# Where the quarter sums of FFN weights are made: DRAM copies against accumulating transfers into SBUF

## The chip, the cores and the metric

The kernel runs on one core of a Trainium2 chip. The metric is the device time of one execution in microseconds (us), in the median of several runs. Of each kernel one execution is also profiled; its span, from the first to the last instruction of the program, is what the views of the profile divide up.

The engines are PE (matrix products, with PEld for the loading of their weights), DVE (elementwise on 128 partitions), ACT (scalar functions, and the casts here), POOL and SP. In this kernel POOL makes almost no arithmetic: it issues DMAs, among them all that add to what lies at their target (`accum_op=add`), and SP issues the plain loads. Each engine executes its own instructions in order, so a DMA that has to wait holds up every later DMA of the engine that issues it.

## The reference

Two layers over 512 latent and 256 context tokens of width 1024, in float32. Layer 0 is windowed attention, layer 1 retention; each is followed by a SwiGLU network of inner width 2816:

```python
def swiglu(h, w_in, w_out):
    gate, up = jnp.split(h @ w_in, 2, axis=-1)
    return (jax.nn.silu(gate) * up) @ w_out

for i in range(DEPTH):
    mx = jnp.split(c_act @ ada_w[i] + ada_b[i], 6, axis=-1)      # latent modulation
    mc = jnp.split(cc_act @ ada_w[i] + ada_b[i], 6, axis=-1)     # context modulation
    h_x = modulate(rms_norm(x, norm1_g[i]), mx[0], mx[1])
    ...                                                          # mixer i, gated residual
    x = x + mx[5] * swiglu(modulate(rms_norm(x, norm2_g[i]), mx[3], mx[4]), ffn_w_in[i], ffn_w_out[i])
    if need_ctx_out:                                             # layer 0 only
        y_ctx = y_ctx + mc[5] * swiglu(...)
```

The change touches the feed-forward network of layer 0 (768 tokens, latent and context side by side) and the modulation vectors of layer 1, which are worked out while it runs.

## The kernel before, in words

Every matrix product is made of three float32r products (high times high, low times high, high times low). So each weight and each activation is split first: ACT casts the high part (L171), DVE subtracts it to get the low part (L172). These two lines appear all over the profile.

**Stages, in order.** Modulation and projections of layer 0 (to about 105 us), attention in 24 blocks, four groups of heads with six blocks each (about 105 to 310), the attention's output projection, the first two column tiles of the feed-forward network in the plain way, then the part around the change: **the run** of gate and up tiles 2 to 21 (about 402 to 705), **the output products** of the same network (705 to 883), then retention and the second network.

**The run.** `w_in` is cut into 22 column tiles of 128 gate and 128 up columns. A tile of gate and up is a 2x2 block matrix: the input `wgu` holds its quarters as gate top (0), gate bottom (1), up top (2), up bottom (3), each 128 x 512 (256 KB). `seven(pos, jobs)` (L1164) computes a tile with 7 products instead of 8, each of 12 matmuls with 384 token columns. For that it needs the quarters, and sums of them. Two sums of raw quarters come from DRAM buffers `gu_sum`: gate top plus up top, loaded to the tile `t1raw` by `load_sum`, and up top plus up bottom, loaded to the left half of a `wraw` tile by `load_up`, whose right half is up bottom. `load_gate` loads both gate quarters. The other sums are DVE additions (L1149, L1155). `t1raw` has one buffer; the three kinds of `wraw` loads go round three buffers, so each load waits on SP until DVE has finished with the buffer's former content.

Where in a tile each load is issued: `load_up(pos + 1)` after the split of the gate tile (`b24`), `load_gate(pos + 2)` after the split of the up tile (`b3`), `load_sum(pos + 2)` after the split of `t1raw` for tile pos + 1. After every second tile `pair_sums` sends four results (`saved`, L1069 and L1071) to DRAM from POOL.

**The sums in DRAM.** `gu_sum` has four batches of five tiles. A batch is two copies (`sum_copy`, L827) and two accumulating DMAs (`sum_add`, L830), 1280 KB each. The output weights need four sums of quarters, `fo_sum`, in two batches of six and five pairs: per batch four copies and four accumulating DMAs (1536 or 1280 KB). `spread` assigns each DMA a turn: turns 0 to 23 are the blocks of attention, -1 is before them, 100 + pos is a tile of the run. The `gu_sum` batches and the first `fo_sum` batch are made before and during attention, the second `fo_sum` batch in the run, from POOL, at tiles 4 (two copies), 6 and 8 (accumulating), 10 (copy), 12 (accumulating), 14 (copy) and 16 (accumulating).

**The order of work.** Outside the run a planner orders the instructions by simulated costs; `after` gives it an order to keep, and puts no wait on the chip. In the run and the output products (`with tc.manual_schedule`, L1453) the order on all engines is the order of the program text.

**The modulation tiles.** Layer 1's modulation is 48 tiles: `ada_next` multiplies a 512 KB weight tile `adaw` with the condition vector on DVE (L284), twice (latent and context) for every second entry of the list from the first on until there are 16 such, once for all others, and `ada_ahead` issues the load of the next tile at once. `adaw` has one buffer, so the load of the next tile waits for the DVE operation on the last, and the next operation waits for that load. In the run the load is issued by SP, in the output products by POOL. `seven` calls two jobs that may be `ada_next`: `jobs[0]` after its third product and `jobs[2]` at the end of the tile. Tiles 5 to 21 have it at `jobs[2]`; all of them but 7, 9, 13 and 17 also have it at `jobs[0]`. That is 30 modulation tiles in the run; the other 18 are done in the output products.

**The output products.** Seven products (prod 0 to 6) of six steps (m 0 to 5), 24 matmuls of 384 columns in a step and 12 in the last. In each step `fo_split` splits the weights and tokens of the step after next on ACT and DVE (2 splits), then the step's matmuls are issued, and then a modulation tile at m = 0, 2 and 4 of prods 0 to 4 and at m = 3 of prods 0 to 3, until none is left. At the end of most products `fo_add` adds the banks to the streams (L1285).

Of the kernel before, what the change touches and what calls it, by code (L numbers as in the profile page):

```python
# [8 lines left out]
F32 = mybir.dt.float32  # L9
# [5 lines left out]
P = 128  # L15
# [9 lines left out]
FFN_GROUPS = (2, 4, 4, 4, 4, 4)  # L25
PAIRS = FT // 2
TURN = [p + PAIRS * j for p in range(PAIRS) for j in range(2)]
GU_BATCH, GU_BATCHES = 5, 4
ROW = 2048
FO_BATCHES = (6, 5)  # L30
RH = 4
# [23 lines left out]
def dit_kernel(ctx, tc, xT, cT, crow, small, consts, masks, tabs0, tabs1, jtab, adaQ, adaN, adaT, wst, wgu, wfo, out):  # L55
    nc = tc.nc
    mult, add, sub = ALU.mult, ALU.add, ALU.subtract
# [38 lines left out]
    by_hand = [False]  # L96

    def after(ins, others):
        for o in others if not by_hand[0] else ():
            tc.add_manual_dep(ins.ins, o.ins.name, order, reason="table set turn")  # L100
# [719 lines left out]

    dp = ctx.enter_context(tc.tile_pool(name="dp", bufs=1, space=bass.MemoryType.DRAM))
    flat = lambda t: t.rearrange("a p n -> (a p n)").rearrange("(x y) -> x y", y=2048)
    gu_sum = [dp.tile([2, GU_BATCH, P, 512], F32, name=f"gu_sum{b}") for b in range(GU_BATCHES)]
    fo_sum = [dp.tile([4, n, P, 512], F32, name=f"fo_sum{b}") for b, n in enumerate(FO_BATCHES)]

    def sum_copy(dst, src, behind):
        after((nc.gpsimd if by_hand[0] else nc.sync).dma_start(flat(dst), flat(src), max_dma_last_dim=ROW), [behind] if behind else [])  # L827

    def sum_add(dst, src, behind):
        after(nc.gpsimd.dma_start(flat(dst), flat(src), accum_op=add, max_dma_last_dim=ROW), [behind] if behind else [])  # L830

    def gu_steps(b):
        rows = slice(2 + b * GU_BATCH, 2 + (b + 1) * GU_BATCH)
        t = gu_sum[b]
        return [lambda a: sum_copy(t[0], wgu[0, rows], a), lambda a: sum_copy(t[1], wgu[2, rows], a),
                lambda a: sum_add(t[0], wgu[2, rows], a), lambda a: sum_add(t[1], wgu[3, rows], a)]

    def fo_steps(b):
        rows = slice(sum(FO_BATCHES[:b]), sum(FO_BATCHES[:b + 1]))
        t = fo_sum[b]  # L840
        return [lambda a: sum_copy(t[3], wfo[0, rows], a), lambda a: sum_copy(t[2], wfo[2, rows], a),
                lambda a: sum_add(t[3], wfo[2, rows], a), lambda a: sum_add(t[2], wfo[3, rows], a),
                lambda a: sum_copy(t[0], t[3], a), lambda a: sum_add(t[0], wfo[3, rows], a),
                lambda a: sum_copy(t[1], t[0], a), lambda a: sum_add(t[1], wfo[1, rows], a)]
# [3 lines left out]
    def spread(steps, turns):  # L848
        for st, n in zip(steps, turns):
            sum_turns.setdefault(n, []).append(st)  # L850

    spread(gu_steps(0), (-1, -1, 0, 1))
    spread(gu_steps(1), (-1, -1, 2, 3))
    spread(gu_steps(2), (4, 4, 6, 7))
    spread(gu_steps(3), (8, 8, 9, 10))
    spread(fo_steps(0), (11, 11, 13, 14, 16, 17, 19, 21))
    spread(fo_steps(1), (104, 104, 106, 108, 110, 112, 114, 116))

    for st in sum_turns[-1]:
        st(keys_end)  # L860
    for piece in make_q(1):
        piece()
    rope_key(kn[2])
# [255 lines left out]
    def ada_next(behind=()):  # L1119

        args = ada_q.pop(0)
        ada_tile(*args, cr, behind, fp, ada_w.pop())
        ada_ahead()
# [12 lines left out]
    def load_up(pos):  # L1136
        u = tile[pos]["u"] = raw_turn()
        nc.sync.dma_start(u[:, R_], wgu[3, pos])
        nc.sync.dma_start(u[:, L_], gu_sum[(pos - 2) // GU_BATCH][1, (pos - 2) % GU_BATCH])

    def load_sum(pos):
        t = tile[pos]["t"] = T(fp, 512, "t1raw", 1)
        nc.sync.dma_start(t, gu_sum[(pos - 2) // GU_BATCH][0, (pos - 2) % GU_BATCH])

    def split_gate(pos):
        t = tile[pos]
# [306 lines left out]
    with tc.manual_schedule(engines=Hand):  # L1453
        by_hand[0] = True
        for pos in range(2, FT):
            jobs = [nothing] * 3
            if pos == 2:
                jobs = [last_sum, gates_negated, nothing]
            elif pos == 3:
                jobs[0] = rows_begin  # L1460
            elif pos == 4:
                jobs[2] = rows_silu
                ada_ahead()
            else:
                cr = row_t[0]
                jobs[2] = ada_next
                if pos not in (7, 9, 13, 17):
                    jobs[0] = ada_next
            if pos == FT - 1:
                def begin():  # L1470
                    fo_split_weights(0)
                    fo_split_tokens(0)
                    fo_split_tokens(1)
                jobs[1] = begin
            end = seven(pos, jobs)
            for st in sum_turns.get(100 + pos, ()):
                st(None)
        fo_y = [bank("Y"), bank("Z"), bank("Z"), bank("Y")]
        o = fo_y
        for i, (prod, m) in enumerate(FO):  # L1480
            if m == 0 and prod:
                o = fo_y if prod in (2, 4) else fo_z if prod == 5 else [bank("X"), bank("X"), pj(384), pj(384)] \
                    if prod in (1, 3) else [bank("Y"), bank("Z"), bank("Z"), bank("Y")]
                if prod == 3:
                    fo_z = o
            if i == 0:
                fo_split_weights(1)
                last_gate(FT - 1)
            if i + 2 < len(FO) and i + 4 != len(FO) and i + 3 != len(FO):
                fo_split(i + 2)  # L1490
            last = i == len(FO) - 2
            fo_step(i, o, prod in (0, 1, 3, 6), last)
            if m == (PAIRS - 1) // 2:
                for args in (((0, 0),), ((0, 0),), ((4, 0, True),), ((4, 1),), ((4, 1, True), (0, 1)), ((4, 0),), ())[prod]:
                    fo_add(o, *args)
            if prod < 5:
                ada_next() if ada_q and (m % 2 == 0 or m == 3 and prod < 4) else None
            elif prod == 5:
                early_sums(m)
            else:  # L1500
                late_sums(m)
            if last:
                break
            if i == 2:
                Q.close()
                H = ExitStack()
                hpool[0] = H.enter_context(tc.tile_pool(name="hR", bufs=1, reuse_waits="tile", side="right"))
                h_rest += [(T(hpool[0], 512, "aq", 11, F32R), T(hpool[0], 512, "aq", 11, F32R)) for _ in range(4)]
                h_first += [T(hpool[0], 512, "aq", 11, F32R) for _ in range(3)]
                off_grid(hpool[0], 16)  # L1510
                h_first.insert(0, T(hpool[0], 512, "aq0", 1, F32R))
                hm += [T(hpool[0], 512, "qk", 8) for _ in range(KT)]
        fo_add(o, 0, 1)
        last_square = last_squares()
        b11.append(split_chunk(b11.pop()))
        by_hand[0] = False
# [778 lines left out]
```

## Time and profile before

| | us |
|---|---|
| median of 3 runs (lowest, highest) | 1723.99 (1723.61, 1726.64) |
| profiled execution | 1723.45 |
| its span | 1721.4 |
| run, from the copy of the first product of tile 2 to that of tile 21 | 404.4 to 693.1 |
| output products 0 to 4 | 705.2 to 834.0 |

Reading: in the views below a row of a group is line, engine, operation, written tile, read tiles, form, how many; then busy us and mean ns of one; then the idle time of the engine just before them and what ended it. A row of waits is engine and what it was to do, `<-` what ended the wait, then us in total, how often, and the longest. A row of windows is from:to, its length, the busy us of PE, PEld, DVE, ACT and POOL with the number of their instructions, the share of full clock granted to PE, the busy share of the 16 DMA engines, and GB/s. PE's busy time is modelled for pipelined matmuls, so lost time is best read as the length of a stretch against that of an undisturbed one with the same work.

### The profile page before, as it was taken

What the parts mean: (1) busy time and instruction counts of PE and PEld (TensorE: products, weight loads), DVE (VectorE), ACT (ScalarE), POOL (GpSimd) and SP (SyncE); (2) the same over time, 40 slices, a digit from 0 to 9 for tenths busy, and PEclk for the clock granted to TensorE, in tenths of its full rate; (3) what the DMA queues carried; (4) which work ended last, traced back from release to release, by engine and by line L of the source; (5) the groups of instructions that cost most, each with busy time, mean ns of one, the idle gap of its engine ahead of it and who ended that gap; (6) DMA issues with size and microseconds to landing.
All of it is one profiled execution on the core that took longest, in us unless ns stands there. A gap on an engine that the chain in (4) does not pass through costs nothing.

```text
span 1721.4 us, 27879 instructions
## 1 busy us (share of the span) xinstructions
PE 1684.6 (98%) x10798; PEld 1523.2 (88%) x10798; DVE 1341.1 (78%) x2395; ACT 891.7 (52%) x1565; POOL 104.5 (6%) x223
## 2 busy tenths in 40 slices
PE   8999999999999999999999999999999999999999
PEld 5878877899999999998988888898898899999997
DVE  6788888797778778776899857757757898877874
ACT  5678878474444334433565535534524564444442
POOL 0011111000101001100000000000000000000000
PEclk9999999999999999999999999999999999999999
DMA  9848967644786777788763624625724323333322
GB/s 382 310 91 195 239 141 190 220 153 141 252 237 231 227 215 227 269 269 286 253 182 72 195 90 120 182 61 132 192 65 100 122 74 113 109 110 111 98 87 86
DMA packets 112035, 293.86 MB, mean 171 GB/s; under 512 B 9520, under 2 KB 20288, under 8 KB 111648
## 3 DMA queue, kind: packets, MB, share of 16 engines
q1 hardware_dynamic: 88960, 227.67, 40.3%
q0 software_dynamic: 22656, 63.90, 16.2%
q8 instruction: 84, 1.38, 0.3%
q10 hardware_dynamic: 288, 0.52, 0.1%
q14 instruction: 47, 0.39, 0.1%
HBM read 274.82 MB, written 61.28 MB: 195 GB/s over the span
## 4 chain that ended last, share of the span: by engine, by line
PE 44%; DVE 6%; DMA 3%; issue 1%; ACT 1%; POOL 0%; DVEq 0%; ACTq 0%; SPq 0%; POOLq 0%
PE Y L971 6%; PE Z L1597 6%; PE Z L971 3%; PE Y L1586 3%; PE pj L154 2%; PE pj L156 2%; PE pj L155 2%; DMA adaw<-in_adaT_dram 2%; PE pj L1597 2%; PE X L971 2%; PE X L1586 1%; DVE wlo L172 1%; DMA wraw<-in_wst_dram 1%; PE X L1597 1%; PE Z L1266 1%
## 5 line engine op out<-in xcount | busy, mean ns | idle before, releaser
L171 ACT CAST whi<-wraw 128x1024 fp32r<-128x1024 f32 (+1 forms) x284 | 294.3, 1040 | 314.3 <-PE Y L971 70.6
L172 DVE TENSOR_TENSOR wlo<-wraw,whi 128x1024 fp32r<-128x1024 f32 (+1 forms) x284 | 342.4, 1209 | 102.1 <-ACT whi L171 101.0
L971 PE MATMUL Y<-aq,whi 128*128 128x384 f32 x640 | 172.8, 335 | 0.0
L284 DVE CUSTOM_DVE_ANT_0 y<-adaw,crow,small_sb 128x1024 bf16<-128x1024 f32 x64 | 82.1, 1283 | 59.0 <-DMA adaw<-in_adaT_dram 58.4
L971 PEld LDWEIGHTS Y<-aq,whi 128*128 128x128 f32 x640 | 116.7, 188 | 0.0
L971 PE MATMUL Y<-aq,wlo 128*128 128x384 f32 x320 | 107.8, 337 | 8.6 <-DVE wlo L172 8.6
L1597 PE MATMUL Z<-whi,sA 128*128 128x512 f32 x256 | 80.6, 392 | 0.0
L108 ACT ACTIVATE pr<-pr,stat,qs 128x513 f32<-128x513 f32 (+2 forms) x96 | 74.1, 774 | 11.3 <-DVE stat L734 11.3
L154 PE MATMUL pj<-ax,whi 128*128 128x512 f32 x176 | 69.2, 393 | 0.5 <-DVE res L263 0.3
L971 PEld LDWEIGHTS Y<-aq,wlo 128*128 128x128 f32 x320 | 60.2, 188 | 10.5 <-DVE wlo L172 10.5
L156 PE MATMUL pj<-ax,whi 128*128 128x512 f32 x176 | 68.7, 390 | 0.0
L155 PE MATMUL pj<-ax,wlo 128*128 128x512 f32 x176 | 68.6, 390 | 0.0
L971 PE MATMUL Y<-sA,whi 128*128 128x256 f32 x304 | 58.3, 277 | 0.0
L263 DVE SCALAR_TENSOR_TENSOR res<-pj,mod,res 128x512 f32<-128x512 f32 (+1 forms) x64 | 45.3, 713 | 16.6 <-PE pj L156 16.6
L753 PE MATMUL pT<-const_sb,pr 128*128 128x128 f32 x352 | 56.4, 285 | 1.8 <-DVE pr L744 1.1
L728 DVE CUSTOM_DVE_ANT_0 pr<-S,mask,qs 128x256 f32<-128x256 f32 (+1 forms) x96 | 53.3, 567 | 5.3 <-PE S L727 4.4
L1597 PEld LDWEIGHTS Z<-whi,sA 128*128 128x128 f32 x256 | 48.0, 188 | 10.5
L971 PE MATMUL Y<-hx,whi 128*128 128x256 f32 x304 | 56.4, 277 | 0.0
L1266 PE MATMUL Y<-aq,whi 128*128 128x384 f32 x176 | 53.4, 340 | 1.6 <-DVE aq L172 1.4
L1266 PE MATMUL Z<-aq,whi 128*128 128x384 f32 x176 | 51.5, 334 | 0.0
L753 PEld LDWEIGHTS pT<-const_sb,pr 128*128 128x128 f32 x352 | 41.2, 145 | 11.0 <-issue 4.3
L1597 PE MATMUL Z<-wlo,sA 128*128 128x512 f32 x128 | 50.5, 395 | 0.0
(602 smaller groups left out, 5089.4 us busy)
## 6 DMA issues: line engine op xcount, KB each, us to landing
wraw<-in_wst_dram SPq DMA_DIRECT2D x157, 512.0 KB, 3.7
adaw<-in_adaT_dram SPq DMA_DIRECT2D x35, 512.0 KB, 3.7
op<-saved SPq DMA_DIRECT2D x35, 384.0 KB, 5.4
saved<-op POOLq DMA_DIRECT2D x33, 384.0 KB, 4.1
wraw<-in_wgu_dram SPq DMA_DIRECT2D x24, 512.0 KB, 4.5
adaw<-in_adaT_dram POOLq DMA_DIRECT2D x21, 512.0 KB, 4.2
gu_sum<-in_wgu_dram SPq DMA_DIRECT2D x8, 1280.0 KB, 12.6
gu_sum<-in_wgu_dram POOLq DMA_DIRECT2D x8, 1280.0 KB, 12.8
```

The costliest lines, as they stand in the source:

```text
L108: ins = nc.scalar.activation(*args, **kw)
L154: nc.tensor.matmul(o, whi, xhi, start=first, stop=False)
L155: nc.tensor.matmul(o, wlo, xhi, start=False, stop=False)
L156: return nc.tensor.matmul(o, whi, xlo, start=False, stop=last)
L171: after(nc.scalar.copy(hi, t), behind)
L172: return nc.vector.tensor_tensor(lo, t, hi, op=sub)
L284: res.append(nc.vector.tensor_tensor_reduce(junk, w, cr[:, s * 1024:(s + 1) * 1024], 1.0, sm_t[:, C_ADAB + l * 48 + j:C_ADAB + l * 48 + j ...
L753: nc.tensor.transpose(tp[:, a * P:(a + 1) * P], self.pr[(0, 2, 1, 3)[a]][:, ki * P:(ki + 1) * P], ident)
L971: nc.tensor.matmul(o, p, r, start=first and k + i == 0, stop=k == 3 and i == 2, skip_group_check=not first)
L1266: nc.tensor.matmul(o[d], p[:, ws], r, start=first and k + e == 0, stop=k == PAIRS - 1 and e == 2, skip_group_check=True)
L1586: ins = nc.tensor.matmul(o[:, e * SC:(e + 1) * SC], p[:, ws], r, start=first and k + e + i == 0, stop=k == 3 and i == 2, skip_group_check= ...
L1597: ins = nc.tensor.matmul(os[t], p, r, start=first and k + i == 0, stop=k == 3 and i == 2, skip_group_check=by_k or not first)
```

## The change

1. `gu_sum`, its four batches (16 DMAs of 1280 KB) and `gu_steps` are gone. In the run `load_up` and `load_sum` load the raw quarter instead (`wgu[2]` and `wgu[0]`, from SP as before), and a second DMA, from POOL, adds the other quarter (`wgu[3]`, `wgu[2]`) into the tile in SBUF. That makes 40 accumulating DMAs of 256 KB, two a tile.
2. The first `fo_sum` batch moves to turns 0 to 10 and the second to turns 11 to 21, so both are made during attention; all their copies are issued by SP. Nothing of them is left in the run.
3. `ada_next` is called at both jobs of all tiles from 5 on: 34 modulation tiles in the run. In the output products it is called at m = 0, 2 and 4 alone, for the 14 that are left.

```diff
-GU_BATCH, GU_BATCHES = 5, 4
...
-    gu_sum = [dp.tile([2, GU_BATCH, P, 512], F32, name=f"gu_sum{b}") for b in range(GU_BATCHES)]
...
     def sum_copy(dst, src, behind):
-        after((nc.gpsimd if by_hand[0] else nc.sync).dma_start(flat(dst), flat(src), max_dma_last_dim=ROW), [behind] if behind else [])
+        after(nc.sync.dma_start(flat(dst), flat(src), max_dma_last_dim=ROW), [behind] if behind else [])
...
-    def gu_steps(b):
-        rows = slice(2 + b * GU_BATCH, 2 + (b + 1) * GU_BATCH)
-        t = gu_sum[b]
-        return [lambda a: sum_copy(t[0], wgu[0, rows], a), lambda a: sum_copy(t[1], wgu[2, rows], a),
-                lambda a: sum_add(t[0], wgu[2, rows], a), lambda a: sum_add(t[1], wgu[3, rows], a)]
...
-    spread(gu_steps(0), (-1, -1, 0, 1))
-    spread(gu_steps(1), (-1, -1, 2, 3))
-    spread(gu_steps(2), (4, 4, 6, 7))
-    spread(gu_steps(3), (8, 8, 9, 10))
-    spread(fo_steps(0), (11, 11, 13, 14, 16, 17, 19, 21))
-    spread(fo_steps(1), (104, 104, 106, 108, 110, 112, 114, 116))
-
-    for st in sum_turns[-1]:
-        st(keys_end)
+    spread(fo_steps(0), (0, 0, 2, 3, 5, 6, 8, 10))
+    spread(fo_steps(1), (11, 11, 13, 14, 16, 17, 19, 21))
...
         u = tile[pos]["u"] = raw_turn()
         nc.sync.dma_start(u[:, R_], wgu[3, pos])
-        nc.sync.dma_start(u[:, L_], gu_sum[(pos - 2) // GU_BATCH][1, (pos - 2) % GU_BATCH])
+        nc.sync.dma_start(u[:, L_], wgu[2, pos])
+        nc.gpsimd.dma_start(u[:, L_], wgu[3, pos], accum_op=add)
...
         t = tile[pos]["t"] = T(fp, 512, "t1raw", 1)
-        nc.sync.dma_start(t, gu_sum[(pos - 2) // GU_BATCH][0, (pos - 2) % GU_BATCH])
+        nc.sync.dma_start(t, wgu[0, pos])
+        nc.gpsimd.dma_start(t, wgu[2, pos], accum_op=add)
...
                 cr = row_t[0]
-                jobs[2] = ada_next
-                if pos not in (7, 9, 13, 17):
-                    jobs[0] = ada_next
+                jobs[0] = jobs[2] = ada_next
...
-            end = seven(pos, jobs)
-            for st in sum_turns.get(100 + pos, ()):
-                st(None)
+            seven(pos, jobs)
...
             if prod < 5:
-                ada_next() if ada_q and (m % 2 == 0 or m == 3 and prod < 4) else None
+                ada_next() if ada_q and m % 2 == 0 else None
```

## The prediction

> **What bounds the kernel now.** I read the page's top, then the waits of PE, then windows over the two stages that the change touches, and last single tiles.
>
> ```profile
> span 1721.4 us, 27879 instructions
> PE 1684.6 (98%) x10798; PEld 1523.2 (88%) x10798; DVE 1341.1 (78%) x2395; ACT 891.7 (52%) x1565; POOL 104.5 (6%) x223
> ...
> 404.40:693.10 288.70, 280.07 (x1599) 278.13 (x1598) 225.22 (x341) 121.54 (x197) 34.10 (x47) 0.99 0.73 223
> ...
> L1175 ACT COPY hn<-Y x20: 482/482/483, 404.4 to 693.1; 128x384 f32<-128x384 f32 x20
> ```
>
> PE bounds it. The change takes no matmul away, so it can only win back time in which PE waits or runs slow. In the run, one ACT copy (L1175) marks each tile: 20 copies from 404.4 to 693.1 are 19 tiles in 288.7 us, 15.19 each. I compare a tile near the end, when no sum in DRAM is in work any more, with tile 15, in which one is.
>
> ```profile
> 598.79 0.48 ACT L1175 COPY hn<-Y 128x384 f32<-128x384 f32 x1 [0.64 <-PE Y L971]
> ...
> 617.98 0.48 ACT L1175 COPY hn<-Y 128x384 f32<-128x384 f32 x1 [0.64 <-PE Y L971]
> ...
> 649.41 0.48 ACT L1175 COPY hn<-Y 128x384 f32<-128x384 f32 x1 [0.64 <-PE Y L971]
> ...
> 663.97 0.48 ACT L1175 COPY hn<-Y 128x384 f32<-128x384 f32 x1 [0.64 <-PE Y L971]
> ...
> 598.80:618.00 19.20, 16.45 (x86) 16.13 (x85) 14.97 (x22) 6.20 (x11) 0.74 (x1) 0.91 0.47 155
> ...
> 649.40:664.00 14.60, 14.60 (x86) 14.60 (x85) 13.75 (x22) 6.27 (x11) 2.02 (x3) 1.00 0.77 235
> 664.00:678.50 14.50, 14.50 (x85) 14.50 (x84) 11.74 (x18) 6.16 (x10) 0.72 (x1) 1.00 0.62 187
> ```
>
> An undisturbed tile takes 663.97 - 649.41 = 14.56 us; tile 15 takes 19.19. Over 19 tiles the run is 288.7 - 19 x 14.56 = **12.1 us** too long. Part of it is the clock: 0.91 over 19.2 us is 1.7 us lost. What PE waits for, and what that waits for:
>
> ```profile
> PE Y L971 <- DVE wlo L172: 8.6, 6, 2.8
> ...
> DVE y L284 <- DMA adaw<-in_adaT_dram: 23.7, 9, 4.2
> ...
> DMA to landing us min/median/max: 3.6/5.9/8.3
> ...
> fo_sum<-in_wfo_dram POOLq DMA_DIRECT2D x1, 1280.0 KB, 14.2
> ...
> DMA to landing us min/median/max: 3.5/3.8/4.5
> ```
>
> PE waits for the low part of a weight, whose DVE instruction stands behind a modulation operation (L284), which waits for its `adaw` load. The first landing row is of `adaw` from 557 to 574, with an accumulating DMA of `fo_sum` in flight for 14.2 us: 8.3 us at worst. The second is of `adaw` in tiles 18 and 19: 3.8 us. So the `fo_sum` batch in the run is what makes these loads late.
>
> The output products have the same chain without `fo_sum`:
>
> ```profile
> 728.30:757.90 29.60, 26.20 (x135) 25.48 (x134) 20.84 (x28) 9.99 (x13) 2.65 (x5) 0.88 0.77 263
> 757.90:782.70 24.80, 23.76 (x134) 22.87 (x134) 17.91 (x24) 9.99 (x13) 2.12 (x4) 1.00 0.86 289
> 782.70:807.80 25.10, 23.75 (x133) 22.77 (x132) 17.73 (x25) 9.90 (x13) 1.62 (x4) 1.00 0.85 285
> 807.80:834.00 26.20, 24.26 (x134) 22.79 (x133) 19.86 (x29) 9.98 (x13) 1.56 (x3) 1.00 0.79 276
> 834.00:856.70 22.70, 22.70 (x133) 22.65 (x132) 18.54 (x38) 13.87 (x22) 0.00 (x0) 1.00 0.68 223
> ...
> DVE y L284 <- DMA adaw<-in_adaT_dram: 33.6, 14, 4.7
> ...
> PE X L1266 <- DVE wlo L172: 3.7, 2, 3.2
> ...
> 729.56 1.28 DVE L284 CUSTOM_DVE_ANT_0 y<-adaw,crow,small_sb 128x1024 bf16<-128x1024 f32 x1 [4.65 <-DMA adaw<-in_adaT_dram]
> ...
> 730.77 1.22 DVE L172 TENSOR_TENSOR wlo<-wraw,whi 128x1024 fp32r<-128x1024 f32 x1
> ```
>
> These are prods 1 to 5. Prod 5, without modulation tiles, takes 22.7 us; 1 to 4 take 105.7, so 105.7 - 4 x 22.7 = **14.9 us** too long. Prod 1 alone is 6.9 over: at its start PE waits 3.2 us for the low part that comes after a 4.65 us wait for `adaw` (the operation at m = 3), and the clock then stands at 0.88 (0.12 x 29.6 = 3.6 us).
>
> **The change part by part.** *The `fo_sum` batch leaves the run.* With it go the 8 us landings; if nothing takes its place, 12.1 us come back.
>
> *Forty accumulating DMAs enter the run.* None stands in the run of before; the nearest rows are those that add 512 KB into SBUF in the retention stage:
>
> ```profile
> wraw<-in_wst_dram POOLq DMA_DIRECT2D x8, 512.0 KB, 5.6
> ...
> adaw<-in_adaT_dram POOLq DMA_DIRECT2D x21, 512.0 KB, 4.2
> ...
> L1439 POOL DMA_DIRECT2D wraw<-in_wst_dram x8: 853/853/856, 930.3 to 1300.5; - x8
> ...
> L1149 DVE TENSOR_TENSOR wraw<-t1raw,wraw x19: 691/692/694, 411.8 to 686.8; 128x512 f32<-128x512 f32 x19
> L1143 SPq DMA_DIRECT2D t1raw<-gu_sum x18: 326/327/338, 413.4 to 672.6; - x18
> ```
>
> Added bytes cost 5.6 against 4.2 us for a plain load from the same queue. For 256 KB the bounds are the plain 2.8 us of the `t1raw` loads (half of the bytes, no adding; their row of landings stands below) and 5.6; I take 4.2, between them. POOL is busy 0.85 us for each, 34 us in all, on an engine used 6% of the span.
>
> ```profile
> DMA to landing us min/median/max: 2.6/2.8/8.1
> ...
> L172 DVE TENSOR_TENSOR wlo<-wraw,whi 128x1024 fp32r<-128x1024 f32 x7 | 8.6, 1224 | 3.4 <-ACT whi L171 3.4
> L284 DVE CUSTOM_DVE_ANT_0 y<-adaw,crow,small_sb 128x1024 bf16<-128x1024 f32 x6 | 7.7, 1282 | 0.1
> L1155 DVE TENSOR_TENSOR wraw<-wraw 128x512 f32<-128x512 f32 x2 | 1.4, 684 | 0.0
> L1201 DVE TENSOR_TENSOR hn<-Z,hn 128x384 f32<-128x384 f32 x2 | 1.1, 554 | 0.7 <-PE Z L971 0.7
> L284 DVE DVE_READ_ACCUMULATOR2_ANT mod<- 128x1 f32 x6 | 0.5, 83 | 0.0
> ```
>
> The wait that the change adds is POOL's for the landing of the plain load. Behind it on POOL stand the `saved` transfers, read only by the output products, and in tiles 20 and 21 `adaw` loads. The sums' own lateness is covered: the last `t1raw` load is issued at 672.6 and its content first used at 686.8, 14.2 us later, against 2.8 + 5.6 = 8.4. The up tile has about as long (issued at the start of a tile, cast at the start of the next). Were that cover gone, each tile would lose what is missing of it on DVE.
>
> What counts is what the 40 transfers do to the `adaw` loads: bounds 3.8 us (tiles 18 and 19) and 8.3 (beside 1280 KB). 256 KB are a fifth of 1280, and a fifth of the 4.5 between them gives 4.7; some loads also meet `saved`, so I take **4.9**. How much a tile bears follows from DVE's order in a pair of tiles with both jobs, at the prices of tiles 18 and 19. Six modulation operations at 1.28 + 0.08 less an overlap of 0.04 make 7.9. Between them lie, after `jobs[0]`, one `wlo` (1.22), three additions of 512 (0.69) and three of 384 (0.55): 4.9; after `jobs[2]`, two `wlo` and two of 384: 3.5, and in every second tile four more of 384: 5.8. Per stretch the longer of this and the load (plus 0.1 to issue it) counts:
>
> - load 3.8: 4.9 + 3.9 + 4.9 + 5.8 + 7.9 = 27.4, under the 29.1 of two tiles;
> - load 4.9: 5.0 + 5.0 + 5.0 + 5.8 + 7.9 = 28.7, still under it;
> - load 5.6: 30.8, or 1.7 over in each of the 8 pairs of tiles 5 to 20, 13.6 us;
> - load 6.0: 32.3, or 25.6 us over the 8 pairs.
>
> At 4.9 PE waits nowhere on the mean; for single late loads I charge 3 us. Run: 12.1 - 3 = **9.1 us won**.
>
> The Trainium skill (DMA: Bandwidth & Descriptors, Rules for kernel authors) speaks against this step: transfers should be of 1 MiB or more, and its fit under Anatomy of one DMA is 2.0 us plus bytes over 436 GB/s. By that, 40 transfers of 256 KB take 40 x 2.6 = 104 us against 8 x 5.0 = 40 for the `fo_sum` batch. The trace gives 14.2 us for one of those eight beside other traffic; most of the page's fixed part is a delay that occupies no engine, so I go by the rows.
>
> *Four modulation tiles move into the run*, with five operations (50 instead of 45): 6.6 us of DVE, in tiles 7, 9, 13 and 17. Tile 18 has both jobs, DVE 13.75 of 14.60, and loses nothing, so this costs 0; without the cover 6.6. Each also brings its load, counted above.
>
> *The output products lose them.* One link (load 4.2, operation 1.32, issue 0.1) is 5.6 us. Four a product are 22.4 of 22.7, and those at m = 2, 3, 4 are a step (4.1 us) apart. With three, two steps (8.2 us) apart, the links have room. Bounds: all 14.9 us, or, if the products' own weights and tokens are just as late, only the 3.7 us that PE waits for `wlo` on bank X. Nearer the first, since the wait that stands ahead of PE's is for `adaw`: I take **12.5 won**.
>
> *Attention.*
>
> ```profile
> gu_sum<-in_wgu_dram SPq DMA_DIRECT2D x8, 1280.0 KB, 12.6
> gu_sum<-in_wgu_dram POOLq DMA_DIRECT2D x8, 1280.0 KB, 12.8
> ...
> POOL pr L711 <- PE pT L753: 132.0, 23, 12.6
> ...
> 105.00:360.00 255.00, 248.99 (x1716) 204.46 (x1715) 216.84 (x628) 186.10 (x408) 30.20 (x99) 0.99 0.71 177
> ```
>
> 16 DMAs of `gu_sum` leave, 8 of the second `fo_sum` batch come, and SP issues its four copies. The first batch now follows the earlier turns: each of its steps needs the landing of the one before (12.6 to 12.8 us), and behind a waiting POOL DMA stand the copies into `pr` (L711) that the softmax needs. POOL there waits 132 us for PE anyway. PE is idle 6.0 us of 255, so at most 6 come back; one landing that shows through costs 12.8. I take 0.
>
> Sum: 9.1 + 12.5 = 21.6. The profiled execution before was 1723.45 (span 1721.4), 0.5 under the median: 1701.9 for a profiled one, **1702.4** for the median.
>
> **The rivals.**
>
> *The additions slow the modulation loads half-way (5.6 us).* For: the DMA engines are busy 0.77 and 0.62 of tiles 18 and 19 without any sum in work. Against: a slower run also spreads the transfers. The run then loses 13.6 of its 12.1: 1723.99 - 12.5 + 1.5 = 1713.
>
> *They become the bound of the run: slower than before.* Same place, DVE at `jobs[0]` and `jobs[2]`, loads of 6.3 us: 6.4 x 4 + 7.9 = 33.5, 4.4 over in 8 pairs, 35.2 us; 1723.99 - 12.1 - 12.5 + 35.2 = 1735. It decides from about 6.0 (25.6 against the 24.6 won elsewhere). Against: only a 1280 KB transfer has brought loads there so far.
>
> *The output products stay tied to their own loads*: 3.7 won in place of 12.5, 1711. For: DMA share 0.85 there; against: the waits name `adaw`.
>
> *Attention pays one landing:* 1715. *The change does nothing*: DVE with six operations a pair has no room and gives back all that leaves, 1724; against it stand tiles 18 and 19.
>
> **How the numbers follow.** Forecast 0.52 (1697 to 1708); additions half-way 0.17; output products tied 0.12; attention 0.07; nothing 0.04; slower 0.08. A measurement of this kernel can tell about 0.2%, 3.4 us. So faster 0.88, same 0.04, slower 0.08. The range 1695 to 1715 holds the forecast and the three rivals at 1711 to 1715.
>
> **What would show it.** Right: tiles of 14.6 us all along the run, mean `adaw` landings under 5 us, PE's wait for `wlo` in it under 3 us; products 1 to 4 under 24 us each and no stretch with a clock of 0.9. Wrong: DVE waiting for `adaw` in nearly every tile and landings over 5.6; DVE or ACT waiting for `t1raw`; prods 1 to 4 still over 24.5; a new wait of ACT for `pr` in attention.

## The result and the profile after

The changed kernel takes 1702.16 us (median of 4 runs, 1700.69 to 1703.52) against 1724.66 of the kernel before beside it: ratio 0.9868, 95% interval 0.9851 to 0.9885. The forecast was 1702.4 in a range of 1695 to 1715. In a second series, with five runs, it took 1698.44 (1698.09 to 1705.59) against 1721.76: 0.987, interval 0.9848 to 0.9892. So the ratio repeats; a median by itself moves by some 4 us between series, and kernels are compared below within one series or by their ratio.

The page after, its first lines and the rows of the loads the forecast spoke of (us from issue to landing at the end of a row):

```profile
span 1700.6 us, 27957 instructions
PE 1674.5 (98%) x10798; PEld 1519.2 (89%) x10798; DVE 1340.9 (79%) x2395; ACT 893.1 (53%) x1565; POOL 124.6 (7%) x247
...
adaw<-in_adaT_dram SPq DMA_DIRECT2D x39, 512.0 KB, 4.1
saved<-op POOLq DMA_DIRECT2D x33, 384.0 KB, 6.9
wraw<-in_wgu_dram SPq DMA_DIRECT2D x40, 256.0 KB, 5.4
```

The modulation loads of SP land in 4.1 us where they took 3.7; POOL's `saved` transfers take 6.9 where they took 4.1. In the changed file the numbers of the lines are 1 to 14 lower: the copy that marks a tile is L1163, the run's product L957, the modulation operation L283, the low part L171, the output products L1254; the additions by DMA are L1126 (up) and L1131 (`t1raw`).

Where the time came from is read from three windows with the same matrix products in both kernels: the run from marking copy to marking copy, from the last one to the first output product, and output products 0 to 4. First the kernel before (its run stands in the prediction), then the changed one, whose first marking copy also starts at 404.4.

```profile
693.10:705.20 12.10, 12.10 (x72) 12.10 (x71) 10.41 (x16) 5.59 (x9) 1.07 (x2) 1.00 0.83 277
705.20:834.00 128.80, 121.07 (x661) 116.73 (x661) 92.36 (x125) 51.06 (x62) 12.47 (x23) 0.97 0.83 282
```

```profile
404.40:684.10 279.70, 277.44 (x1599) 276.56 (x1597) 230.83 (x352) 122.56 (x196) 58.28 (x75) 1.00 0.80 233
684.10:698.70 14.60, 12.46 (x72) 12.14 (x72) 10.71 (x15) 5.60 (x9) 1.06 (x2) 1.00 0.75 260
698.70:813.30 114.60, 114.60 (x661) 114.32 (x660) 86.32 (x115) 51.12 (x62) 10.28 (x19) 1.00 0.88 299
...
721.80:744.70 22.90, 22.90 (x134) 22.90 (x134) 17.28 (x23) 9.99 (x13) 1.58 (x3) 1.00 0.90 297
...
790.50:813.30 22.80, 22.80 (x133) 22.80 (x132) 16.73 (x25) 9.90 (x13) 1.06 (x2) 1.00 0.77 270
```

The run goes from 288.7 to 279.7 (9.0 won), the stretch behind it from 12.1 to 14.6 (2.5 lost), the products from 128.8 to 114.6 (14.2 won); their sum, 20.7, is the difference of the spans (20.8) but for rounding. The clock of the products rises from 0.97 to 1.00, and prods 1 to 4, 22.9 or 22.8 each, are within 0.2 us of prod 5.

### The profile page after: what moved, and what is told of

Read it like the earlier page. It is cut to its first block, busy times and chain, and to the rows that moved or that the text cites. A ratio compares the mean times of both kernels' runs of the same rounds, so it can differ in the third digit from the quotient of the medians.

```text
span 1700.6 us, 27957 instructions
## 1 busy us (share of the span) xinstructions
PE 1674.5 (98%) x10798; PEld 1519.2 (89%) x10798; DVE 1340.9 (79%) x2395; ACT 893.1 (53%) x1565; POOL 124.6 (7%) x247
## 4 chain that ended last, share of the span: by engine, by line
PE 51%; DVE 5%; DMA 2%; ACT 1%; issue 1%; DVEq 0%; ACTq 0%; SPq 0%
PE Z L1581 7%; PE Y L957 6%; PE Z L957 3%; PE Y L1570 3%; PE Y L1254 2%; PE Z L1254 2%; PE pj L153 2%; PE pj L155 2%; PE pj L154 2%; PE pj L1254 2%; PE X L1254 2%; PE pj L1581 2%; PE X L957 1%; PE X L1570 1%; DMA wraw<-in_wst_dram 1%; DVE wlo L171 1%
## 5 line engine op out<-in xcount | busy, mean ns | idle before, releaser
L171 DVE TENSOR_TENSOR wlo<-wraw,whi 128x1024 fp32r<-128x1024 f32 (+1 forms) x284 | 342.4, 1209 | 104.7 <-ACT whi L170 102.2
L957 PE MATMUL Y<-aq,whi 128*128 128x384 f32 x640 | 172.4, 334 | 0.0
L957 PEld LDWEIGHTS Y<-aq,whi 128*128 128x128 f32 x640 | 116.6, 188 | 0.0
L957 PE MATMUL Y<-aq,wlo 128*128 128x384 f32 x320 | 107.4, 335 | 4.4 <-DVE wlo L171 4.4
L283 DVE CUSTOM_DVE_ANT_0 y<-adaw,crow,small_sb 128x1024 bf16<-128x1024 f32 x64 | 82.1, 1283 | 37.1 <-DMA adaw<-in_adaT_dram 36.4
L957 PEld LDWEIGHTS Y<-aq,wlo 128*128 128x128 f32 x320 | 60.1, 188 | 5.6 <-DVE wlo L171 5.6
L957 PE MATMUL Y<-sA,whi 128*128 128x256 f32 x304 | 58.1, 277 | 0.0
L957 PE MATMUL Y<-hx,whi 128*128 128x256 f32 x304 | 56.3, 277 | 0.0
L1254 PE MATMUL Y<-aq,whi 128*128 128x384 f32 x176 | 52.9, 337 | 0.0
L1254 PE MATMUL Z<-aq,whi 128*128 128x384 f32 x176 | 51.4, 334 | 0.0
```

Source lines behind the costliest of these rows:

```text
L171: return nc.vector.tensor_tensor(lo, t, hi, op=sub)
L283: res.append(nc.vector.tensor_tensor_reduce(junk, w, cr[:, s * 1024:(s + 1) * 1024], 1.0, sm_t[:, C_ADAB + l * 48 + j:C_ADAB + l * 48 + j ...
L957: nc.tensor.matmul(o, p, r, start=first and k + i == 0, stop=k == 3 and i == 2, skip_group_check=not first)
L1254: nc.tensor.matmul(o[d], p[:, ws], r, start=first and k + e == 0, stop=k == PAIRS - 1 and e == 2, skip_group_check=True)
```

## What holds PE up in the run, by tiles

What remains of the run's excess is 3.1 us (279.7 - 19 x 14.56). Of it 2.8 us sit in two tiles. DVE's timeline in the changed kernel, three of its waits for `adaw` (in brackets: the wait and what ended it):

```profile
564.05 1.28 DVE L283 CUSTOM_DVE_ANT_0 y<-adaw,crow,small_sb 128x1024 bf16<-128x1024 f32 x1 [2.10 <-DMA adaw<-in_adaT_dram]
...
594.02 1.28 DVE L283 CUSTOM_DVE_ANT_0 y<-adaw,crow,small_sb 128x1024 bf16<-128x1024 f32 x1 [2.96 <-DMA adaw<-in_adaT_dram]
...
625.34 1.28 DVE L283 CUSTOM_DVE_ANT_0 y<-adaw,crow,small_sb 128x1024 bf16<-128x1024 f32 x1 [4.53 <-DMA adaw<-in_adaT_dram]
```

ACT's timeline, the marking copies of tiles 13 to 18:

```profile
564.83 0.48 ACT L1163 COPY hn<-Y 128x384 f32<-128x384 f32 x1 [0.64 <-PE Y L957]
579.39 0.48 ACT L1163 COPY hn<-Y 128x384 f32<-128x384 f32 x1 [0.64 <-PE Y L957]
593.95 0.48 ACT L1163 COPY hn<-Y 128x384 f32<-128x384 f32 x1 [0.64 <-PE Y L957]
609.13 0.48 ACT L1163 COPY hn<-Y 128x384 f32<-128x384 f32 x1 [0.64 <-PE Y L957]
623.69 0.48 ACT L1163 COPY hn<-Y 128x384 f32<-128x384 f32 x1 [0.64 <-PE Y L957]
640.44 0.48 ACT L1163 COPY hn<-Y 128x384 f32<-128x384 f32 x1 [0.64 <-PE Y L957]
```

A wait of 2.10 us costs the tile behind it nothing (579.39 - 564.83 = 14.56), one of 2.96 costs 0.6 (15.18), one of 4.53 costs 2.2 (16.75). So some 2.4 us of one wait are slack, and what is over that reaches PE one to one. The slack is smaller where two modulation operations (latent and context) stand behind the wait: in tile 9 of the kernel before, with the operations at 507.44 and 508.76 us, a wait of 2.98 us costs 1.8, so 1.1 us are slack there. The load in the even tile is the late one: it is issued there 7.1 us behind the marking copy, while POOL's transfers of the `saved` results and of the sums are in flight. Over the run the landings of these loads have a wide spread; the view of the tile `adaw` in the changed kernel, who waited for it (us, times) and the landings (the 15th of these waits, 4.76 us, stands behind the run, in tile 21):

```profile
  DVE y L283: 27.3, 15
...
DMA to landing us min/median/max: 3.5/4.2/9.1
```

Averaged over all loads issued between the first and the last marking copy, the landing is 4.89 us in the changed kernel (32 loads) and 4.81 in the kernel before (28 loads): the mean tells nothing. What differs is how many land late. In the kernel before, the even tiles 6 to 16 have landings of 7.9, 8.3, 7.6, 8.3, 9.5 and 8.8, and the tiles behind them are too long by 1.0, 1.8, 0.7, 1.5, 4.6 and 2.3 us: together 11.9 of the 12.1 us. In the changed kernel the landings are 4.9, 7.1, 6.8, 6.6, 7.5 and 9.1, and only the last two cost more than 0.2 us.

## The experiments

**1. The modulation tiles back where they were.** The changed kernel with

```diff
-                jobs[0] = jobs[2] = ada_next
+                jobs[2] = ada_next
+                if pos not in (7, 9, 13, 17):
+                    jobs[0] = ada_next
...
-                ada_next() if ada_q and m % 2 == 0 else None
+                ada_next() if ada_q and (m % 2 == 0 or m == 3 and prod < 4) else None
```

> The change without its third part: 30 modulation tiles in the run and 18 in the output products, as before; sums as in the change. Theory (the output products are tied to the chain of modulation load and operation, four links a product): output products 0 to 4 go back from 114.6 us to about 128, the run stays at 277 to 280 between its first and its last marking copy; time about 1714. Rival (the output products won because the transfers around them became lighter): products 0 to 4 stay under 118 us, time about 1703.

Measured: 1713.15 us, ratio 0.9952 (0.9934 to 0.997). Its run and its products 0 to 4:

```profile
403.30:681.20 277.90, 277.02 (x1598) 276.66 (x1597) 224.15 (x340) 121.59 (x196) 58.34 (x75) 1.00 0.78 228
...
694.50:824.20 129.70, 121.03 (x662) 116.42 (x661) 92.28 (x125) 50.99 (x62) 12.39 (x23) 0.97 0.82 281
```

The products are as long as before (129.7 against 128.8) and their clock is down at 0.97 again, though no `gu_sum` and no `fo_sum` is in work in either. So the whole gain of the products hangs on the modulation tiles, and the gain of the run doesn't.

**2. The same number, one step apart.** The changed kernel with its modulation tiles of the products at m = 2, 3 and 4:

```diff
-                ada_next() if ada_q and m % 2 == 0 else None
+                ada_next() if ada_q and m in (2, 3, 4) else None
```

> The changed kernel, with the modulation tiles of output products 0 to 4 at m = 2, 3 and 4 in place of 0, 2 and 4: as many, one step apart. If their number a product decides (three links of 5.6 us are 16.8 of 22.7 us), products 0 to 4 stay at 114.6 to 117 us and the time at 1702. If it is the distance (a link of 5.6 us against a step of 4.1), each product gets 1 to 3 us longer, products 0 to 4 take 119 to 127 us and the time is 1707 to 1714.

Measured: 1709.27 us, ratio 0.9946 (0.9928 to 0.9964). Its products:

```profile
693.80:818.00 124.20, 118.43 (x662) 114.22 (x661) 83.40 (x113) 51.15 (x62) 10.28 (x19) 1.00 0.79 269
```

And of its waits in this stretch DVE's for `adaw`:

```profile
DVE y L283 <- DMA adaw<-in_adaT_dram: 39.0, 9, 6.3
```

The same wait is 8.1 us in the changed kernel's products. With as many tiles the products get 9.6 us longer (124.2 against 114.6), at full clock, though their loads land sooner (4.2 us in the median against 5.0): the distance decides. Two steps of 4.1 us give a link of 5.6 room, one step does not. Other places of the three tiles in a product were not tried.

**3. The output weights' batch back in the run.** The changed kernel with

```diff
-    spread(fo_steps(1), (11, 11, 13, 14, 16, 17, 19, 21))
+    spread(fo_steps(1), (104, 104, 106, 108, 110, 112, 114, 116))
...
             seven(pos, jobs)
+            for st in sum_turns.get(100 + pos, ()):
+                st(None)
```

and the copies of these turns issued by POOL, as before.

> The change, but with the second batch of output weight sums back in the run, from POOL, at tiles 4 to 16 as before. Theory (1280 KB transfers beside a modulation load make it land at 8 us and DVE late): the run goes from 279.7 us to 292 or more, single modulation loads land after more than 8 us; time 1714 to 1730. Rival (the 256 KB additions already set the landings, what else is in flight hardly matters): the run stays under 284 us, time 1702 to 1706.

Measured: 1723.6 us (10 runs, 1714.59 to 1730.57), ratio 1.0011 (0.9988 to 1.0034). Its profiled execution, one of the shorter ones (1715.64):

```profile
404.10:697.70 293.60, 284.37 (x1599) 278.99 (x1597) 231.23 (x352) 121.85 (x196) 65.89 (x83) 0.99 0.88 258
...
712.30:826.90 114.60, 114.60 (x661) 114.32 (x661) 86.06 (x115) 51.09 (x62) 10.32 (x19) 1.00 0.88 298
```

And the landings of its `adaw` loads in the run:

```profile
DMA to landing us min/median/max: 3.4/5.0/10.1
```

The products keep their gain; the run is 293.6, longer than before the change (288.7). The landings are 5.4 on the mean over its 32 loads. Additions and the batch together undo, in the median, all that the rest of the change brings. The profiled execution is 8 us shorter than the median; where these 8 us go in the longer ones is not shown.

**4. The same batch in pieces.** The kernel before, each of the batch's eight transfers of 1280 KB cut into five of 256 KB, spread over the same tiles (`fo_pieces` makes the eight steps of `fo_steps` for one pair of tiles at a time):

```diff
-    spread(fo_steps(1), (104, 104, 106, 108, 110, 112, 114, 116))
+    pieces = fo_pieces(1)
+    for i in range(8):
+        for k in range(FO_BATCHES[1]):
+            sum_turns.setdefault(104 + (5 * i + k) * 14 // 40, []).append(pieces[8 * k + i])
```

> The kernel before, with the second batch of output weight sums still in the run of gate and up tiles (tiles 4 to 17), but each of its eight transfers of 1280 KB cut into five of 256 KB and spread evenly, so that the same bytes are copied and added in the run. If the late modulation loads come from one long transfer in flight (12.8 to 14.2 us at a time), the landings fall from 8.3 us at worst to about 5, the run from 288.7 to 279 to 283 us, and the time to 1712 to 1716. If the bytes decide, whatever their pieces, the run stays at about 288 us and the time at 1722.

Measured: 1716.83 us against 1721.13, ratio 0.9978 (0.9968 to 0.9989). Its run:

```profile
405.20:687.40 282.20, 277.93 (x1599) 276.57 (x1598) 224.95 (x341) 121.60 (x196) 54.69 (x79) 1.00 0.73 228
```

And the landings of `adaw` in it:

```profile
DMA to landing us min/median/max: 3.4/3.9/8.3
```

Half of each theory. The run wins 6.5 of its 12.1 us in this profile, as the long transfer's theory wanted, but the worst landing did not fall to 5, and 5.6 us stay, so the length of one transfer is not the whole cause; the time is just above the 1712 to 1716 expected of that theory. The pieces are also spread more evenly over the tiles than the whole transfers were, and the two effects are not told apart. The Trainium skill (DMA: Bandwidth & Descriptors, Rules for kernel authors) asks for 1 MiB or more per DMA for the highest bandwidth. Here cutting 1280 KB into 256 KB made the kernel slightly faster (ratio 0.9978) at the same DMA share of the run (0.73 in both): what costs time in this stage is not the bandwidth of the batch but the loads of another stream that land late.

**5. No additions.** The changed kernel without the forty accumulating DMAs, so that the sums of gate and up lack their second part:

```diff
-        nc.gpsimd.dma_start(u[:, L_], wgu[3, pos], accum_op=add)
...
-        nc.gpsimd.dma_start(t, wgu[2, pos], accum_op=add)
```

> The change without its 40 accumulating DMAs of 256 KB: the two sums of gate and up quarters are left out, so the raw quarter stands in their place and the output differs. Theory (these additions make the modulation loads of the even tiles land at 7 to 9 us and are all that is left of PE's waits in the run): run 276.6 to 277.5 us, 12.1 to 13 from there to the output products, time 1697 to 1698. Rival (six modulation operations in two tiles are too many for DVE with or without the additions): run stays at 279 to 280, time 1702.

Measured: 1696.15 us, ratio 0.986 (0.9835 to 0.9885). Its run:

```profile
403.70:680.50 276.80, 276.80 (x1599) 276.77 (x1599) 233.68 (x355) 121.61 (x196) 26.63 (x40) 1.00 0.64 202
```

276.8 is 0.2 over 19 x 14.56, the run without any stall (the first of its tiles takes 14.70 in every kernel here).

**6. All sums in DRAM.** The kernel before with both `fo_sum` batches in attention and the modulation tiles as in the change, `gu_sum` kept; no addition into SBUF enters the run:

```diff
-    spread(fo_steps(1), (104, 104, 106, 108, 110, 112, 114, 116))
+    spread(fo_steps(1), (12, 12, 14, 15, 17, 18, 20, 22))
...
-                jobs[2] = ada_next
-                if pos not in (7, 9, 13, 17):
-                    jobs[0] = ada_next
+                jobs[0] = jobs[2] = ada_next
...
-                ada_next() if ada_q and (m % 2 == 0 or m == 3 and prod < 4) else None
+                ada_next() if ada_q and m % 2 == 0 else None
```

> The kernel before with the second batch of output weight sums moved to attention (turns 12 to 22) and the modulation tiles as in the change; the gate and up sums stay in DRAM. Nothing is added in the run. Theory (the run is relieved by the leaving of the batch, not by where the gate and up sums are made): run 276.6 to 277.5 us, output products as in the change, time 1696 to 1699 if attention hides 32 sum transfers. Rival (attention cannot hide a third batch): the first marking copy of the run comes 5 us or more after 404.4, time 1702 or more.

Measured: 1697.84 us, ratio 0.9871 (0.9845 to 0.9897). As much as the change wins, without its additions: attention holds six batches about as well as two. It is run again in 9.

**7. One modulation tile later.** The changed kernel without `jobs[2]` in tile 20; its tile goes to the end of the list, into the output products:

```diff
-                jobs[0] = jobs[2] = ada_next
+                jobs[0] = ada_next
+                if pos != 20:
+                    jobs[2] = ada_next
```

> The changed kernel without the second modulation tile in tile 20, which goes to the end of the queue, into the output products. If its load, which lands 9 us after its issue, is what holds tile 21 up, the stretch from the last marking copy to the output products falls from 14.6 to 12.1 us, products 0 to 4 stay at 114.6, and the time is 1699 to 1700. If tile 21 waits for its own weights, the stretch stays at 14.6 and the time at 1702.

Measured: 1697.79 us, ratio 0.9876 (0.986 to 0.9891). What is late without this edit, in the changed kernel at the end of tile 20 and the start of tile 21, in POOL's timeline:

```profile
670.22 0.85 POOL L1131 DMA_DIRECT2D t1raw<-in_wgu_dram  x1 [5.56 <-DVE wlo L171]
...
675.54 0.91 POOL L1126 DMA_DIRECT2D wraw<-in_wgu_dram  x1 [1.33 <-DMA wraw<-in_wgu_dram]
676.94 0.56 POOL L274 DMA_DIRECT2D adaw<-in_adaT_dram  x1 [0.48 <-DVE mod L283]
```

and in DVE's:

```profile
678.42 0.68 DVE L171 TENSOR_TENSOR blo<-t1raw,bhi 128x512 fp32r<-128x512 f32 x1
686.00 1.28 DVE L283 CUSTOM_DVE_ANT_0 y<-adaw,crow,small_sb 128x1024 bf16<-128x1024 f32 x1 [4.76 <-DMA adaw<-in_adaT_dram]
687.21 0.08 DVE L283 DVE_READ_ACCUMULATOR2_ANT mod<- 128x1 f32 x1
687.21 1.22 DVE L171 TENSOR_TENSOR wlo<-wraw,whi 128x1024 fp32r<-128x1024 f32 x1
```

POOL waits 0.48 us for DVE's last modulation operation and issues the load at 676.94, beside four `saved` transfers and the two sums; it lands 9 us later, DVE's operation starts at 686.00, and the low part that PE needs in tile 21 stands behind it. With the edit the stretch behind the run is 12.1 us, as expected. The time is below the 1699 to 1700 expected, but by its ratio this kernel is no faster than the changed one (0.9868); the two are compared side by side in 9.

**8. Plain transfers in place of the additions.** The changed kernel with the forty transfers left where they are, of the same bytes, that overwrite instead of adding:

```diff
-        nc.gpsimd.dma_start(u[:, L_], wgu[3, pos], accum_op=add)
+        nc.gpsimd.dma_start(u[:, L_], wgu[3, pos])
...
-        nc.gpsimd.dma_start(t, wgu[2, pos], accum_op=add)
+        nc.gpsimd.dma_start(t, wgu[2, pos])
```

> The changed kernel, whose forty additions into the gate and up tiles are plain transfers: the same source, size, queue, place and waits, but they overwrite in place of adding, so the gate and up sums are left out. If it is the adding itself that makes the modulation loads of the run late, the run falls from 279.8 to about 277 us, tile 21 no longer stalls, and the time is 1696 to 1698, as it was without these transfers. If it is their bytes and their place on the queue, the run stays at 279 to 281, tile 21 stalls, and the time stays at 1701 to 1703.

Measured: 1696.47 us, ratio 0.987 (0.9855 to 0.9885), the run 276.8, which by the expectation speaks for the adding. But the kernel of 2, whose run is the same code as the changed kernel's, also has a run of 276.7 in its profile. So the 3.1 us had to be tried for chance.

**9. Four of them on one chip, four or five runs of each.** The changed kernel again, and those of 7, 8 and 6.

> The changed kernel once more, on the same chip as the next three. Its run took 279.8 us in one profile, and 276.8 us in a profile of the kernel with steps 2, 3 and 4, whose run is the same code: so the stalls in tiles 15, 17 and 21 are not in every execution. If they belong to most executions, it is 3 to 6 us slower than the next three (a median of 1700 to 1704 where they have 1696 to 1699). If they were chance, all four lie within 2 us of one another.

> The changed kernel without the second modulation tile in tile 20, once more. If its load is what holds tile 21 up, 2 to 3 us under the changed kernel beside it, and the last marking copy stands 12.1 us ahead of the output products again; if not, as fast as that within 1 us.

> The changed kernel with plain transfers in place of the forty additions (the gate and up sums are left out), once more. If the adding itself costs the run, 3 to 6 us under the changed kernel beside it; if only the bytes and the queue count, within 1 us of it.

> The kernel before with both batches of output weight sums in attention and the modulation tiles as in the change, the gate and up sums still made in DRAM, once more. If attention carries all six batches at no cost and the run is better off without additions, 3 to 6 us under the changed kernel beside it (1696 to 1698); if the additions cost nothing on the mean, or attention pays for the bytes, within 2 us of it.

| kernel | median us (lowest, highest) | ratio to before (interval) |
|---|---|---|
| changed | 1698.44 (1698.09, 1705.59) | 0.987 (0.9848, 0.9892) |
| one tile later | 1696.71 (1695.33, 1697.49) | 0.985 (0.9831, 0.9869) |
| plain transfers | 1697.27 (1695.98, 1700.6) | 0.9858 (0.9837, 0.9879) |
| all sums in DRAM | 1699.36 (1697.46, 1700.04) | 0.9865 (0.9845, 0.9885) |

The changed kernel's second profile, its run and the stretch behind it:

```profile
403.20:680.00 276.80, 276.80 (x1599) 276.77 (x1599) 231.96 (x352) 122.61 (x196) 58.44 (x75) 1.00 0.80 236
680.00:693.90 13.90, 12.40 (x72) 12.09 (x71) 10.33 (x15) 5.60 (x9) 1.07 (x2) 1.00 0.74 258
```

The landings of `adaw` in that run:

```profile
DMA to landing us min/median/max: 3.4/4.1/8.3
```

The kernel with one tile later:

```profile
403.80:680.60 276.80, 276.80 (x1599) 276.77 (x1598) 233.05 (x353) 121.69 (x197) 58.33 (x75) 1.00 0.81 236
680.60:692.70 12.10, 12.10 (x72) 12.10 (x71) 8.69 (x13) 5.55 (x9) 0.53 (x1) 1.00 0.78 272
```

The kernel with plain transfers:

```profile
403.60:680.40 276.80, 276.80 (x1599) 276.77 (x1598) 232.57 (x353) 121.57 (x197) 45.78 (x75) 1.00 0.71 236
```

The stalls in tiles 15 and 17 are not there the second time: here the even tiles' landings that DVE waits for stay at or under 6.3 us (the 8.3 is tile 20's). Of the five profiles whose run has this code up to tile 20, only the first has them: 279.7 us against 276.7 (experiment 2), 277.0 (experiment 7), 276.8 and 276.8. So they were chance, and the reading of 8 by the length of the run falls: with plain transfers the kernel is 1.2 us faster in overlapping ranges, not 3 to 6. Nor do the sums in DRAM gain 3 to 6; they are 0.9 behind. All three are within 2 us of the changed kernel, as the theory of chance has it. So where the sums of gate and up are made, in DRAM or in SBUF, makes no difference that these runs can tell; what wins is that the `fo_sum` batch leaves the run and that the modulation tiles stand further apart.

The stall of tile 21 is no chance. The five profiles of kernels with additions and `jobs[2]` in tile 20 have 14.6, 13.9, 13.3, 14.6 and 13.1 us behind the run; all others, the two with plain transfers among them, 12.1 or 12.2. That is what the adding, beside the bytes, costs in these profiles. All five runs of the kernel with one tile later (1695.33 to 1697.49) lie under all five of the changed kernel; the medians are 1.7 us apart, 0.1%, a little less than the 2 to 3 us expected, and it has the lowest median of the kernels here that compute the whole. The intervals of the two ratios overlap, so the size of the gain is not settled.

Not settled either: why a load lands at 9.1 us in one execution and at 6.1 in another of the same code.

## Why the prediction was right, by its own steps

**The run, 12.1 us too long.** Right in cause: without the batch 9.0 or, in the second profile, 11.9 come back, and with the batch in the changed kernel 16.8 more are lost than in that profile (293.6 against 276.8). Only "one long transfer" is too narrow, by experiment 4. The 3 us charged for single late loads are 3.1 in the first profile and 0.2 in the second: a size that varies between executions, not the step.

**The landing of 4.9 as the term that decides.** The mean came out at 4.89 (4.4 in the second profile), and the argument behind it still failed. The kernel before has 4.81 and loses 12.1 us; by the pair-of-tiles sum it should have lost nothing. That sum takes every load at the mean, but time is lost by a single wait of more than 2.4 us (1.1 ahead of two operations), that is, in the changed kernel, by a landing above some 7.2 in an even tile. "Mean landing under 5" was therefore a sign that held before the change as well. What held of the list of signs: tiles of 14.6 but for three (9 at 14.73, 15, 17) and, from the waits between the first and the last marking copy, PE's for `wlo` under 3 us:

```profile
PE Y L957 <- DVE wlo L171: 2.3, 2, 1.9
...
DVE y L283 <- DMA adaw<-in_adaT_dram: 22.6, 14, 4.5
...
POOL t1raw L1131 <- DMA t1raw<-in_wgu_dram: 74.8, 11, 10.4
...
ACT bhi L170 <- DMA t1raw<-in_wgu_dram: 7.1, 8, 1.2
```

DVE waits for `adaw` as long as before (22.6 against 23.7 us) in 14 waits instead of 9, and PE a quarter as long (2.3 against 8.6): shorter waits, most of them within the slack.

**The additions' own price, 4.2 between 2.8 and 5.6.** Missed, at the upper bound or above it: in the median the 256-KB additions take 5.7 us (`t1raw`, L1131) and 6.2 us (up, L1126), in the second profile 5.9 and 5.5. The landings of these two lines in the changed kernel:

```profile
DMA to landing us min/median/max: 3.9/5.7/7.6
```

```profile
DMA to landing us min/median/max: 4.2/6.2/8.9
```

The cover is smaller than argued too. I counted from SP's issue of the plain load at 672.6 to DVE's use at 686.8, 14.2 us; but ACT casts the tile earlier, at 685.1, 12.5 us after that issue. And the plain load takes longer than the 2.8 us I took: in the changed kernel it lands in 4.6 us in the median, and POOL issues the last `t1raw` addition at 670.22 (experiment 7), 5.8 us after the plain load's start. That addition lands in 7.1 us, and ACT's cast waits 1.1 us for it and starts at 677.4: the cover was 6.1 us. That is why ACT's wait for `t1raw`, a sign on my list of wrongs, is there (7.1 us, at most 1.2 at once). None of it reached PE: the free step was free with little to spare.

**POOL behind the waiting addition.** The prediction named the `adaw` loads that stand there in tiles 20 and 21 and gave them no price. The lost term is at this place, 2.5 us in the first profile and 1.0 to 2.5 in five, but in the first profile it is not the queue that makes it: POOL has issued the addition and waits for DVE when it comes to this load (experiment 7). It is the landing. In tile 20 this load lands in 6.8 to 9.0 us in the seven profiles with additions, in 5.6 and 6.3 with plain transfers, and in 4.6 to 5.7 in the five with neither.

**Four tiles more in the run at 0.** Right: the run reaches 276.8 with 34 of them, and experiment 1 with 30 has 277.9.

**Output products, 12.5 won.** The mechanism was right, the size small: 14.2, near the upper bound of 14.9, so the products' own weights and tokens kept almost nothing; experiment 1 gives the whole 14.2 back, and 0.9 more, through the modulation tiles alone. The two grounds named together, three a product and two steps apart, are told apart by experiment 2: number alone wins 4.6 (128.8 to 124.2), distance the other 9.6.

**Attention at 0.** Right. POOL's wait for the attention's products before it copies, in the changed kernel:

```profile
POOL pr L710 <- PE pT L752: 136.5, 24, 13.9
```

The window from 105 us to its first marking copy:

```profile
105.00:404.00 299.00, 292.68 (x2082) 247.22 (x2081) 257.57 (x706) 218.25 (x478) 29.81 (x101) 0.99 0.59 154
```

That wait was 132.0 us before, and the copy starts at 404.4 in both kernels, with a DMA share of 0.69 before and 0.59 after. With all six batches (experiment 6) the copy starts at 404.6 the first time and at 406.2 the second, with a share of 0.82: at most some 2 us for sixteen transfers more.

**The rivals.** Additions that slow the loads half-way did come about, but only beside the batch (experiment 3: mean 5.4, 16.8 us over), where the time was 1723.6. Additions as the bound of the run, the products tied to their own loads, attention paying a landing, and no effect are each excluded by the windows above.

The sum of the steps, 9.1 + 12.5 = 21.6, against 9.0 - 2.5 + 14.2 = 20.7: one term 1.7 short, one missed. That these two nearly cancel, and that the 3 us charged for late loads were met by the first profile and not by the second, is luck. The two large steps were right, but the 0.2 us between forecast and median are no measure of how well the sizes were known.

## What to carry to other kernels

Judge a prefetch by its late landings and by the slack of the instruction behind it, not by its mean: 4.8 and 4.9 us on the mean were 12 us and 3 us lost. Keep a long or bulky background transfer out of stages in which a single-buffered load gates an in-order engine, and put such loads further apart than one link of load and operation takes. When additions enter a stage, price the landing of each load that flies beside them, the last one of the stage too. And test each part of a change alone: one that brings nothing can hide behind the others.

## What was not expected of the hardware

An addition by DMA into SBUF occupies the DMA engines more than twice as long as a plain transfer of the same bytes. With 36 such transfers in the run the DMA share over 276.8 us is 0.80, with 36 plain ones 0.71, without them 0.64 (the rows of 9 and 5): 0.16 x 276.8 / 36 = 1.23 us on all 16 engines for an addition of 256 KB, 0.07 x 276.8 / 36 = 0.54 for a plain one; the shares are rounded to 0.01, so each may be off by some 0.08. The packets (first number; then MB) rise as well. POOL's queue in the changed kernel's second profile, and in that of the plain one:

```profile
q0 software_dynamic: 21248, 56.57, 15.2%
```

```profile
q0 software_dynamic: 18688, 56.57, 13.3%
```

For the same bytes 2560 packets more, 64 for each of the forty additions. By the Trainium skill (DMA: Bandwidth & Descriptors, Anatomy of one DMA) the variable part of a DMA's time is its bytes over 436 GB/s, for 256 KB an estimate of 0.60 us, beside a fixed part of some 2.0 us. The plain transfers agree with 0.54 us, so the fixed part occupies no engine here, as the prediction took it; the 1.23 us for adding are twice the estimate. The longer occupancy moved the median by 1.2 us in overlapping ranges (experiment 9): but for tile 21 PE waited for none of it in the second profile.
